# The instruction scheduler's simulator, exchanged under a two-layer diffusion block on one core

## Chip, cores and metric

The program runs on one core of a Trainium2 chip (trn2). The metric is the device time of one execution in microseconds (us). A run's time is that of the whole execution; a profiled execution has also a span, from its first to its last recorded instruction. The engines are PE (TensorE, matmuls; PEld is its weight load), DVE (VectorE), ACT (ScalarE), POOL (GpSimd) and SP (SyncE, which issues nearly all DMAs here). Each engine works through one list of instructions in the order in which the program holds them.

## The reference, cut to what matters

256 latent tokens `x` and 256 context tokens `ctx`, 1024 channels, go through two layers. In the last layer the context is only carried as far as its keys and values.

```python
for l in range(DEPTH):                                   # 2
    mod_x = silu(c) @ w_ada[l] + b_ada[l]                # 9 modulation vectors, also for ctx
    x = ffn_half(x, mod_x, 0, ...); cx = ffn_half(cx, ...)
    u_x, u_c = modulated_norm(x, ...), modulated_norm(cx, ...)
    q, k, v, f, cg, sc, g = split_in(u_x @ w_in[l])      # 18 tiles of branches, 32 of gates
    attn = latent_attention(...)                         # q/k RMS norm, rotary, softmax
    x = x + mod_x[5] * merge_branches(attn, f, cg, sc, g, lw)
    if not last: cx = cx + mod_c[5] * merge_branches(...)
    x = ffn_half(x, mod_x, 2, ...)                       # D_FF 2816
    if not last: cx = ffn_half(cx, ...)
return rmsnorm(x, final_norm_g)
```

`merge_branches` adds four gated branches: attention, a Fourier mixer, a convolution of 31 taps, a short gated convolution.

## The kernel before

Activations stand with channels on the 128 partitions and tokens along the free axis: 512 columns while both streams are carried (`NB = 2`: stream 0 latent, stream 1 context), 256 in the last layer's mixer and last FFN (`NB = 1`).

**Products.** Each f32 operand is split in a high and a low part. `mm3` (L192) issues three matmuls, at L193, L194 and L195, for high x high, high x low and low x high. `wblock` (L183) brings one weight block of 128 x 1024: a DMA by SP into a ring `raw` of 4 (L185), a cast by ACT into a ring `whi` of 6 (L187), a subtraction by DVE into a ring `wlo` of 6 (L189). `split` (L197) does the same for activations (L199 on ACT, L200 on DVE).

**Stages.** `ffn` (L559) runs first and second projection in three parts; `down` (L511) adds the result to the residual `xt`. In the last part its last two output tiles are computed stream by stream: stream 0's matmuls, then stream 1's, each followed by `residual` (L374 on DVE), `square_in` (L369 on ACT, L370 on DVE, into `acc`) and `nxt.stat(s)`. That statistic is `x_rstd`: narrow matmuls (L225) that sum squares over the channels, an inverse root of 11 small DVE instructions (`rsqrt`, L208 to L217), and a transpose that spreads it (L233). `Norm.part` (L415) then makes the next stage's input (L421 on DVE, L425 on ACT, L426 on DVE). The next stage's first products run by halves (`project(..., halves=True)`), so that stream 0 can begin while stream 1 is normalised. There are four such boundaries with two streams: FFN to mixer and mixer to FFN in layer 0, FFN to FFN between the layers, FFN to mixer in layer 1. Behind the layer 1 mixer stands a `LateNorm`, whose inverse root is multiplied in only behind the matmuls.

**Work between.** `ada_later` (L297) computes the later modulations on DVE (L331, L333, four instructions for each block of `w_ada`, ring of 2) and sums them with PE (L315). It is a generator that `filler` steps on inside FFN and merge. In the mixer, `attention` (L868) is another generator; the matmuls of scores are L888, the softmax is L892 (DVE), L895 (DVE), L900 (ACT), L903 and L904 (DVE), the transposes are L915 (PE) and L919 (ACT), the product with the values L932 (PE). `pump` and `tap` step attention and the convolution (L703, DVE) on between the gate products of `merge` (L991).

**What sets the order.** The Python program is traced in program order. Behind the trace, a list scheduler makes the order of every engine: it runs the program in a simulator, and whenever the simulated engine can take an instruction, it gives it the one that stands earliest in the program among those whose inputs are finished and whose ring slots are free in that simulation. The order found is written into the program and is the order on the chip; times of the simulation are not kept, only the order and the choice of ring slots, and semaphores are then assigned to it. Where the simulation and the chip differ, an engine on the chip can stand before an instruction that is not ready while a later one would be. Only the first piece of the program is fixed by hand, and only for two engines: `with tc.manual_schedule(engines={PE, SP})` at L1073, which takes in the loads of `x`, the first modulations and the first FFN products. Its ACT and DVE instructions are ordered by the scheduler as elsewhere.

The change touches the line that makes the context (L1264):

```python
    with tile.TileContext(nc) as tc:
        hybrid_block(tc, aps, out)
```

## Time and profile before

| what | value |
|---|---|
| median of 3 runs | 2047.06 us (2044.32 to 2049.98) |
| the profiled execution, its own time | 2047.93 us |
| its span | 2046.1 us |
| mean granted PE clock | 0.995 |
| instructions | 28,259 |
| DMA | 294.10 MB |

Busy time of an engine is the time in which at least one of its recorded instructions ran. A window row gives, for one stretch of the span, each engine's busy time with the number of instructions in brackets, then the granted clock of PE (1.00 is the full one), the share of time that the 16 DMA engines were busy, and their GB/s. In a timeline row the number in square brackets is the idle time of the engine ahead of the instruction and what ended it. In the chain of waits, each piece is the work that released the one behind it.

### The profile page before, as it was taken

Reading aid. Unit: us, or ns where it says so; the run is one execution under the profiler, and the core shown is the slowest. Engines: PE = TensorE matmul, PEld = TensorE weight load, DVE = VectorE, ACT = ScalarE, POOL = GpSimd, SP = SyncE. Lnnn points to the kernel's source line nnn. Section 1 sums busy time; section 2 is a strip of 40 time slices with the busy share of each in tenths; the row PEclk is TensorE's granted clock in tenths of the full one; section 3 lists DMA queues with packets and bytes.
Section 4 is the critical chain, followed back from the end, with each engine's and each line's share of the span. In section 5 each row is a group of like instructions: output and inputs, shape, how many; then the busy total and the mean of one; then the engine's idle time right before and its main releaser. Section 6 shows DMA issues by size and latency. Waiting matters only on the chain.

```text
span 2046.1 us, 28259 instructions
## 1 busy us (share of the span) xinstructions
PE 2006.9 (98%) x11074; PEld 1712.0 (84%) x11074; DVE 1376.6 (67%) x2470; ACT 737.0 (36%) x1142; POOL 5.1 (0%) x30
## 2 busy tenths in 40 slices
PE   6999999999999999999999999999999999999998
PEld 4878878888887778888887888888888999899997
DVE  5996697576766657768777657932424878767665
ACT  3322322333254442432222233222223545655443
POOL 0000000000000000000000000000000000000000
PEclk9999999999999999999999999999999999999999
DMA  8765566333222225246656533623323454446663
GB/s 295 232 204 168 159 212 193 111 96 98 83 86 84 78 70 167 75 153 192 198 160 192 165 101 109 220 83 95 111 87 101 140 165 140 139 125 205 181 182 92
DMA packets 83493, 294.10 MB, mean 144 GB/s; under 512 B 9504, under 2 KB 10144, under 8 KB 83360
## 3 DMA queue, kind: packets, MB, share of 16 engines
q1 hardware_dynamic: 83072, 292.07, 45.9%
q8 instruction: 87, 1.43, 0.3%
q14 instruction: 46, 0.38, 0.1%
q10 hardware_dynamic: 288, 0.23, 0.0%
HBM read 289.11 MB, written 1.05 MB: 142 GB/s over the span
## 4 chain that ended last, share of the span: by engine, by line
PE 95%; DVE 2%; ACT 1%; DMA 1%; issue 1%; DVEq 0%; ACTq 0%; SPq 0%
PE mm L193 30%; PE mm L194 30%; PE mm L195 29%; PE aux L932 1%; PE aux L888 1%; PE aux L915 1%; PE aux L315 1%; DVE wlo L189 1%; PE aux L775 1%; PE aux L225 0%; ACT whi L187 0%; PE aux L800 0%; DMA ada<-in_w_ada 0%; ACT s L900 0%; PE aux L260 0%
## 5 line engine op out<-in xcount | busy, mean ns | idle before, releaser
L193 PE MATMUL mm<-s,whi 128*128 128x512 f32 (+2 forms) x3354 | 1168.7, 349 | 4.8 <-ACT s L1003 1.4
L194 PE MATMUL mm<-s,whi 128*128 128x512 f32 (+2 forms) x3354 | 1165.3, 348 | 1.4 <-DVE s L200 1.2
L195 PE MATMUL mm<-s,wlo 128*128 128x512 f32 (+2 forms) x3354 | 1163.2, 347 | 0.0
L187 ACT CAST whi<-raw 128x1024 fp32r<-128x1024 f32 (+1 forms) x408 | 420.2, 1032 | 1051.4 <-PE mm L194 874.1
L189 DVE TENSOR_TENSOR wlo<-raw,whi 128x1024 fp32r<-128x1024 f32 (+1 forms) x408 | 487.1, 1199 | 347.1 <-ACT whi L187 331.3
L193 PEld LDWEIGHTS mm<-s,whi 128*128 128x128 f32 x3354 | 635.0, 190 | 101.1 <-ACT s L577 8.5
L194 PEld LDWEIGHTS mm<-s,whi 128*128 128x128 f32 x3354 | 636.6, 190 | 80.9 <-DVE s L200 2.1
L195 PEld LDWEIGHTS mm<-s,wlo 128*128 128x128 f32 x3354 | 636.2, 190 | 78.4 <-issue 0.8
L333 DVE SCALAR_TENSOR_TENSOR s<-ada,cw,s 128x512 f32<-128x512 f32 x448 | 307.4, 744 | 22.3 <-DMA ada<-in_w_ada 22.1
L374 DVE SCALAR_TENSOR_TENSOR xt<-mm,modG,xt 128x256 f32<-128x256 f32 x192 | 85.5, 478 | 132.9 <-PE mm L195 132.6
L199 ACT CAST s<-s 128x512 fp32r<-128x512 f32 (+1 forms) x104 | 59.4, 572 | 77.1 <-DVE s L587 48.9
L703 DVE SCALAR_TENSOR_TENSOR s<-pad,dw_h,s 128x512 f32<-128x512 f32 (+1 forms) x120 | 73.8, 615 | 2.1
L200 DVE TENSOR_TENSOR s<-s,s 128x512 fp32r<-128x512 f32 (+1 forms) x104 | 64.8, 623 | 2.0 <-ACT s L199 2.0
L425 ACT ACTIVATE s<-s,mod 128x256 fp32r<-128x256 f32 x80 | 39.4, 507 | 41.9 <-DVE s L421 41.8
L587 DVE TENSOR_TENSOR s<-s,mm 128x512 f32<-128x512 f32 x66 | 44.8, 680 | 1.2 <-ACT s L577 0.7
L892 DVE TENSOR_REDUCE sm<-aux 128x1 f32<-128x512 f32 (+1 forms) x48 | 28.6, 595 | 24.5 <-PE aux L888 24.4
L900 ACT ACTIVATE s<-aux,sm,sm 128x512 f32<-128x512 f32 (+1 forms) x48 | 34.0, 708 | 26.2 <-DVE sm L895 26.1
L467 DVE TENSOR_TENSOR s<-mm,s 128x256 f32<-128x256 f32 x44 | 18.1, 419 | 37.3 <-PE mm L195 37.3
L577 ACT ACTIVATE s<-mm 128x512 f32<-128x512 f32 x66 | 38.9, 590 | 1.2 <-PE mm L195 1.2
L426 DVE SCALAR_TENSOR_TENSOR s<-s,mod,s 128x256 fp32r<-128x256 f32 x80 | 37.2, 476 | 1.7 <-ACT s L425 1.7
L1024 DVE SCALAR_TENSOR_TENSOR s<-s,mm 128x512 f32<-128x512 f32 x48 | 32.7, 682 | 6.8 <-PE mm L195 5.9
L369 ACT ACTIVATE s<-xt 128x256 f32<-128x256 f32 x70 | 26.8, 410 | 28.2 <-DVE xt L374 28.1
(128 smaller groups left out, 723.0 us busy)
## 6 DMA issues: line engine op xcount, KB each, us to landing
raw<-in_w SPq DMA_DIRECT2D x208, 512.0 KB, 4.3
ada<-in_w_ada SPq DMA_DIRECT2D x144, 512.0 KB, 3.8
raw<-in_w_in SPq DMA_DIRECT2D x100, 512.0 KB, 3.7
raw<-in_w SPq DMA_DIRECT2D x64, 448.0 KB, 3.9
raw<-in_w_br SPq DMA_DIRECT2D x20, 512.0 KB, 3.6
raw<-in_w_o SPq DMA_DIRECT2D x16, 512.0 KB, 4.1
xt<-in_xt SPq DMA_DIRECT2D x4, 512.0 KB, 6.2
s<-s SPq DMA_DIRECT2D x16, 128.0 KB, 2.2
```

The lines of the kernel that those rows point to most:

```text
L187: nc.scalar.copy(hi[:, :n], raw[:, :n])
L189: nc.vector.tensor_tensor(out=lo[:, :n], in0=raw[:, :n], in1=hi[:, :n], op=ALU.subtract)
L193: nc.tensor.matmul(ps, lhsT=wh, rhs=xh, start=first, stop=False)
L194: nc.tensor.matmul(ps, lhsT=wh, rhs=xl, start=False, stop=False)
L195: nc.tensor.matmul(ps, lhsT=wl, rhs=xh, start=False, stop=last)
L199: nc.scalar.copy(hi[:, :n], src)
L200: nc.vector.tensor_tensor(out=lo[:, :n], in0=src, in1=hi[:, :n], op=ALU.subtract)
L333: nc.vector.scalar_tensor_tensor(out=t, in0=src, scalar=cs, in1=t, op0=ALU.mult, op1=ALU.add)
L374: nc.vector.scalar_tensor_tensor(out=xt[:, m, c], in0=ps[:, c], scalar=G[:, m, s : s + 1], in1=xt[:, m, c], op0=ALU.mult, op1=ALU.add,)
L425: nc.scalar.activation(hi[:, c], z, AF.Identity, bias=B[:, k, s : s + 1])
L587: nc.vector.tensor_tensor(out=h[:, :T], in0=s[:, :T], in1=ps[:, :T], op=ALU.mult)
L703: nc.vector.scalar_tensor_tensor(out=ov, in0=h[:, :NB, j : j + S], scalar=dw_h[:, l, i, j : j + 1], in1=ov, op0=ALU.mult, op1=ALU.add,)
```

## The change

One argument is given to the context; the body of the kernel is the same. With it, the scheduler drives another simulator: the library's timeline model of the devices in place of its default core simulator, each with its own durations and its own account of when an engine can take an instruction. The tracing, the priorities (the places in the program), the ring sizes and the region at L1073 are as they were.

```diff
@@ -1261,7 +1261,7 @@
     out = nc.dram_tensor("out", (P, KD, S), F32, kind="ExternalOutput").ap()
-    with tile.TileContext(nc) as tc:
+    with tile.TileContext(nc, schedule_with_timeline_sim=True) as tc:
         hybrid_block(tc, aps, out)
```

## Rows read from the trace of the kernel before

**Rows 1.** The page: busy time of the engines, with shares of the span.
```profile
PE 2006.9 (98%) x11074; PEld 1712.0 (84%) x11074; DVE 1376.6 (67%) x2470; ACT 737.0 (36%) x1142; POOL 5.1 (0%) x30
```

**Rows 2.** The page: the chain that ended last, shares of the span by engine.
```profile
PE 95%; DVE 2%; ACT 1%; DMA 1%; issue 1%; DVEq 0%; ACTq 0%; SPq 0%
```

**Rows 3.** Windows of the whole span, cut at the stage boundaries (columns in the first line).
```profile
core 0: us, PE busy (x) PEld busy (x) DVE busy (x) ACT busy (x) POOL busy (x), PEclk, DMA share, GB/s
0.00:45.00 45.00, 29.39 (x197) 19.11 (x198) 23.84 (x65) 17.60 (x33) 2.32 (x16) 1.00 0.80 291
45.00:404.00 359.00, 357.78 (x1633) 290.04 (x1634) 273.10 (x416) 99.50 (x134) 1.04 (x2) 1.00 0.60 188
404.00:604.00 200.00, 198.91 (x1019) 166.73 (x1018) 137.99 (x263) 74.51 (x116) 0.58 (x8) 1.00 0.29 89
604.00:850.00 246.00, 242.20 (x1187) 195.22 (x1185) 158.88 (x335) 103.89 (x193) 0.00 (x0) 0.99 0.33 99
850.00:862.00 12.00, 10.15 (x81) 9.66 (x81) 10.52 (x35) 6.20 (x13) 0.00 (x0) 1.00 0.13 44
862.00:1219.00 357.00, 356.15 (x1672) 292.95 (x1671) 252.31 (x387) 99.26 (x132) 0.00 (x0) 1.00 0.54 165
1219.00:1235.00 16.00, 14.58 (x106) 13.90 (x105) 12.45 (x47) 7.18 (x13) 0.00 (x0) 0.89 0.21 67
1235.00:1590.00 355.00, 355.00 (x1669) 295.34 (x1669) 174.91 (x256) 98.55 (x133) 0.00 (x0) 1.00 0.37 116
1590.00:1605.00 15.00, 13.57 (x96) 12.73 (x94) 11.67 (x44) 6.87 (x13) 0.00 (x0) 0.89 0.24 69
1605.00:1800.00 195.00, 192.68 (x1476) 180.76 (x1476) 157.91 (x319) 108.81 (x193) 1.17 (x4) 1.00 0.49 151
1800.00:2034.00 234.00, 234.00 (x1943) 233.73 (x1942) 157.66 (x293) 113.72 (x172) 0.00 (x0) 1.00 0.54 163
2034.00:2046.10 12.10, 2.51 (x17) 1.82 (x15) 5.30 (x18) 0.89 (x3) 0.00 (x0) 0.69 0.23 87
```

**Rows 4.** Windows of 10 us in the layer 0 mixer, around PE's longest stop there.
```profile
650.00:660.00 10.00, 6.34 (x28) 4.99 (x27) 6.47 (x12) 6.10 (x12) 0.00 (x0) 0.80 0.40 118
660.00:670.00 10.00, 10.00 (x50) 7.01 (x49) 5.50 (x18) 4.55 (x12) 0.00 (x0) 0.85 0.01 2
```

**Rows 5.** Timeline, 648 to 664 us, all engines: start, length, what, idle before.
```profile
651.29 1.05 ACT L187 CAST whi<-raw 128x1024 fp32r<-128x1024 f32 x1 [5.75 <-PE mm L194]
...
653.01 0.78 ACT L900 ACTIVATE s<-aux,sm,sm 128x512 f32<-128x512 f32 x1
...
655.55 0.66 PE L915 MATMUL aux<-ident,s 128*128 128x128 f32 x4 [2.72 <-DVE s L904]
```

**Rows 6.** Timeline of PE at the first two-stream boundary, 396 to 413 us.
```profile
404.64 0.61 PE L225 MATMUL aux<-ones_d,acc 128*128 128x1 f32 x4
...
408.55 0.28 PE L195 MATMUL mm<-s,wlo 128*128 128x256 f32 x1
408.75 1.05 PE L315 MATMUL aux<-s,ones_w 128*32 128x512 f32 x2
...
412.37 0.73 PE L193 MATMUL mm<-s,whi 128*128 128x256 f32 x4 [0.33 <-ACT s L425]
```

**Rows 7.** The chain of waits at that boundary, in order of time.
```profile
408.75 1.05 ACT whi L187
...
409.82 1.23 DVE wlo L189
411.05 0.35 DVE acc L370
```

**Rows 8.** Who waited for whom, ACT: total, times, longest.
```profile
ACT whi L187 <- PE mm L194: 874.1, 224, 17.3
```

**Rows 9.** The page's groups by line: the modulations' multiply-adds.
```profile
L333 DVE SCALAR_TENSOR_TENSOR s<-ada,cw,s 128x512 f32<-128x512 f32 x448 | 307.4, 744 | 22.3 <-DMA ada<-in_w_ada 22.1
```

**Rows 10.** Window in the first FFN of layer 1, nothing but wide products.
```profile
1350.00:1400.00 50.00, 50.00 (x222) 41.40 (x221) 15.48 (x20) 10.86 (x13) 0.00 (x0) 1.00 0.29 92
```

## The prediction

> **What bounds the kernel now.** I read the busy times first: PE is busy for 2006.9 us of the span of 2046.1, so it stands for only 39.2 us, while DVE has 67% and ACT 36% [rows 1]. The chain that ended last says the same, PE 95% [rows 2]. So the order of instructions can bring back no more than what PE stands, and what it loses in clock. The windows cut at the stage boundaries show where that is [rows 3]. The first stretch holds 45.00 - 29.39 = 15.6 us of it and the last one 12.10 - 2.51 = 9.6. The ten between hold 1.22 + 1.09 + 3.80 + 1.85 + 0.85 + 1.42 + 0 + 1.43 + 2.32 + 0 = 14.0 us. In the four long FFN stretches (45 to 404, 862 to 1219, 1235 to 1590, 1800 to 2034) PE stands 2.1 us out of 1305: there the reader is to see an engine that nothing holds up.
>
> **What the stops look like.** The longest is in the layer 0 mixer, and it is one of order. ACT reached a weight cast (L187) at 651.29 after 5.75 us of standing, since the cast needed a ring slot that PE's own matmuls had to free; the softmax of the attention (L900) stood behind it in ACT's list, and PE had already come to the transposes (L915) that need that softmax: 2.72 us [rows 5]. All in all PE lost 10.00 - 6.34 = 3.66 us in those 10 us, and the granted clock was 0.80 and then 0.85 over two windows of 10 us, another (0.20 + 0.15) x 10 = 3.5 us: 7.2 us for one misplaced hand-over [rows 4]. The casts stand 874.1 us behind PE, 224 times, up to 17.3 us [rows 8]; that costs something only where work that PE soon needs is queued behind one. The granted clock fell to 0.89 at two of the boundaries as well, 16 x 0.11 + 15 x 0.11 = 3.4 us [rows 3]. So the middle holds at most 14.0 + 3.5 + 3.4 = 20.9 us that a better order could give back.
>
> **The change, part by part.** It removes and adds no computation and no transfer: the same matmuls, casts and DMAs. What it can move is the place of each in the lists of ACT, DVE, PE, SP and POOL. POOL's 30 instructions (5.1 us) carry no weight [rows 1]. Five places count.
>
> - *The start.* PE's and SP's order is written by hand up to L1073's end; the stop of PE there stands ahead of the first products. Only ACT and DVE can be re-ordered, and they stand half empty (17.6 and 23.8 of 45.0 us) [rows 3]. I cost it at nothing, hidden by the wait for the loads of `x`; the cover lacks only if DVE put other work ahead of the square sums, one instruction of 744 ns [rows 9].
> - *The end.* One serial chain from the last matmul to the output, with nothing to choose between: nothing.
> - *The long FFN stretches.* Weight blocks run ahead through rings of 4 and 6, so a cast or a split that moves by a microsecond is covered by the blocks already there. Cost: nothing; gain at most 2.1 us. SP's list can swap a load of `w_ada` with one of a weight block; what covers that is the same rings, DMA being busy 0.37 to 0.60 of the time here [rows 3].
> - *The four boundaries with two streams.* This is the term. Before, the statistic of stream 0 (L225) was put into the middle of stream 1's matmuls, at 404.64, as soon as its sum was ready; stream 1 went on until 408.55, summing of modulations (L315) filled in from 408.75, and the next stage began at 412.37 [rows 6]. The slack is thus all used. If the new simulation lets PE's list take in the rest of stream 1's matmuls, which are ready, ahead of the statistic, it comes 408.55 - 404.64 = 3.9 us later, and everything of the next stage with it. The trace of before shows no boundary in that order, so I bound it: at least nothing or a small gain (an order better than before's could win back the 1.09 to 1.85 us that a boundary's stretch now stands), at most 3.9 us of standing and 3.5 us of clock behind it, as after the stop of 3.66 us [rows 4]. I take 3.9, near the middle, since the shorter stops at the boundaries took 1.7 us of clock or none [rows 3]. Four boundaries: **15.6 us**. Waiting on the statistic behind it are DVE's L421 and, through ACT's L425, PE's first products.
> - *The attention's hand-overs.* PE passes scores to DVE and ACT and takes the probabilities back. In the mixers PE stands 3.80 and 2.32 us in all [rows 3]. A new order moves these stops rather than ends them: I take nothing, between minus 7.2 us (the one large stop gone) and twice plus 7.2 (one more in each mixer) [rows 4].
>
> The sum is 15.6 us on the profiled execution: 2047.93 + 15.6 = 2063.5. That execution lies 0.87 us above the median shown, so the median becomes 2047.06 + 15.6 = **2062.7 us**.
>
> **Where the skill speaks for more.** In a stretch of nothing but wide products PE is busy 50.00 us of 50.00 and its weight load 41.40; 222 matmuls make 225 ns for each, against 213 ns for 512 columns at 2.4 GHz [rows 10]. PE waits for nothing in that stretch, so no order can shorten it. The Trainium skill (Trainium Kernel Development and Optimization, Performance Expectations) calls matmul busy time a bad measure of the distance to the roofline and the weight load's share a good one. By that reading 84% would leave 16% to win and the 20.9 us above would be no ceiling; the rows here do not bear that out for an exchange of order, and no term hangs on it.
>
> **The rivals.**
>
> *Faster.* The new simulation stands nearer to the chip and its order has fewer misplaced hand-overs. For it: at the boundary a cast of 1.05 us and a split of 1.23 stand ahead of the sum that the statistic waits for [rows 7], and at 651 the cast stood ahead of the softmax [rows 5]; an order that knew better would put both behind. Against it: the ceiling of 20.9 us, of which part is the latency of a serial chain that no order removes. I price it at half: 10.4 us, 2036.6. It decides if PE's stops at 650 and at 850, 1220 and 1590 are gone.
>
> *No change.* The two simulators order the same wherever it matters, or the change does nothing at all: 2047.1, within 0.3% (6 us, about what a measurement of this kernel can tell from no change). For it: 98% busy, and an order that follows the program wherever everything is ready.
>
> *Slower by more.* Work that is ready early but needed late is put ahead of a chain that PE waits for. The modulations' multiply-adds are that work: four of 744 ns make 3.0 us of DVE for each block [rows 9], and DVE is busy 10.52 of 12 and 12.45 of 16 us at boundaries [rows 3]. One block ahead of one hop at each boundary, with the 3.9 us, makes 4 x (3.9 + 3.0) = 27.6; two further stops in the mixers at 7.2 make 14.4: 42 us, 2089. It decides if DVE's L333 stands in the timeline between L374 and L208 at the boundaries.
>
> **How the numbers follow.** The forecast (the statistics late, 2062.7) has a chance of 0.32, the heavier rival 0.18, no change 0.25, faster 0.25. Why half the chance to lose: the gain has a ceiling of 1% and needs most of the stops mended, while the loss has none and needs one new stop at a place where the slack is used up. Faster by over 0.3% is then 0.25, within 0.3% 0.25, slower 0.50. The range goes from the middle of the faster case, 2036, to a little above the heavier one, 2092: half of the faster case and a part of the heavier lie outside, about 0.2. The slower cases alone run from 2053 to 2092.
>
> **What would show it.** Right: busy PE time about as now, and its idle time up by some 16 us, nearly all in the windows around the four boundaries; L225 of stream 0 behind the last of stream 1's matmuls in PE's timeline; the FFN stretches still full. Wrong: PE idle below 30 us and the mixer's stop at 650 gone (faster); the timeline of PE at the boundaries as now (no change); new stops of over 3 us with a granted clock below 0.9 in the mixers, or DVE's multiply-adds between residual and statistic (the heavier rival). Wrong altogether would be a stop in the FFN stretches: a weight ring run dry, casts or splits ordered too late, DMA waits in the chain.

## The result, and the profile after

| what | before | after |
|---|---|---|
| median of 4 runs each | 2048.52 us (2044.32 to 2050.73) | 2122.91 us (2121.66 to 2128.43) |
| ratio, 95% interval | | 1.0371 (1.0356 to 1.0386) |
| the profiled execution, its own time | 2047.93 us | 2121.66 us |
| its span | 2046.1 us | 2119.9 us |
| mean granted PE clock | 0.995 | 0.981 |

The change makes the kernel 3.7% slower, some 75 us. The forecast was slower by 15.6 us, with a range that ended at 2092: the direction was right and the size far too small.

The page of the kernel after, busy time of the engines (it answers to [rows 1]):

```profile
PE 2033.5 (96%) x11074; PEld 1731.4 (82%) x11074; DVE 1383.4 (65%) x2470; ACT 733.0 (35%) x1142; POOL 5.1 (0%) x30
```

Each engine's count of instructions is that of before. PE stood for 2119.9 - 2033.5 = 86.4 us against 39.2 before: 47.2 us more. The rest of the span's 73.8 us is PE's own busy time, 26.6 us more for the same 11074 matmuls, at a mean granted clock of 0.981 instead of 0.995.

Windows of 10 us of the kernel after, at the four boundaries, in the two mixers' worst places, with 50 us of an FFN among them (from 1300) and, as the last row, 20 us around the late norm behind the second mixer (columns as in [rows 3]: PE, PEld, DVE, ACT, POOL, then granted clock, DMA share, GB/s):

```profile
410.00:420.00 10.00, 5.25 (x32) 4.67 (x31) 9.16 (x29) 4.20 (x9) 0.00 (x0) 0.82 0.36 105
420.00:430.00 10.00, 10.00 (x74) 10.00 (x74) 6.95 (x25) 3.12 (x8) 0.00 (x0) 0.84 0.00 0
...
640.00:650.00 10.00, 5.61 (x31) 4.58 (x30) 5.34 (x14) 4.62 (x10) 0.00 (x0) 0.93 0.18 55
650.00:660.00 10.00, 6.42 (x18) 5.13 (x19) 5.73 (x12) 5.25 (x8) 0.00 (x0) 0.56 0.00 0
...
870.00:880.00 10.00, 8.72 (x74) 8.52 (x72) 5.11 (x15) 3.56 (x6) 0.00 (x0) 1.00 0.26 88
880.00:890.00 10.00, 6.81 (x30) 6.43 (x31) 9.01 (x31) 3.52 (x9) 0.00 (x0) 0.53 0.23 69
1250.00:1260.00 10.00, 9.45 (x80) 9.25 (x78) 6.26 (x14) 3.26 (x7) 0.00 (x0) 1.00 0.23 59
1260.00:1270.00 10.00, 5.89 (x26) 5.51 (x27) 9.04 (x32) 4.26 (x10) 0.00 (x0) 0.66 0.26 100
1300.00:1350.00 50.00, 50.00 (x209) 37.76 (x209) 46.10 (x68) 11.50 (x15) 0.00 (x0) 1.00 0.67 212
1630.00:1640.00 10.00, 7.49 (x63) 7.29 (x62) 6.22 (x17) 3.56 (x6) 0.00 (x0) 1.00 0.36 107
1640.00:1650.00 10.00, 7.54 (x41) 7.17 (x42) 8.54 (x33) 3.52 (x8) 0.00 (x0) 0.66 0.16 52
1790.00:1800.00 10.00, 4.74 (x24) 3.24 (x22) 6.50 (x20) 3.49 (x6) 0.00 (x0) 0.77 0.38 129
1800.00:1810.00 10.00, 9.44 (x59) 9.26 (x60) 7.77 (x19) 6.88 (x16) 0.00 (x0) 0.72 0.01 2
1920.00:1940.00 20.00, 15.20 (x107) 14.78 (x106) 13.38 (x34) 10.18 (x14) 0.00 (x0) 0.83 0.40 129
```

The reader is to see three things. The FFN is as full as before. At the four boundaries (the eight rows from 410, 420, 870, 880, 1250, 1260, 1630 and 1640) PE stands 4.75 + 0 + 1.28 + 3.19 + 0.55 + 4.11 + 2.51 + 2.46 = 18.9 us and the clock takes 10 x (0.18 + 0.16 + 0 + 0.47 + 0 + 0.34 + 0 + 0.34) = 14.9 us. Before, the same places held 1.85 + 1.42 + 1.43 us [rows 3] and 0.7 at the first one (PE was busy 19.34 of the 20 us from 404), 5.4 in all, and 3.4 us of clock [rows 3]. So the boundaries cost 13.5 us more in stops and 11.5 more in clock, 25 us of the span's 73.8. The other 49 us are what is left, nearly all of it in the mixers. The late norm behind the second one has 8 of them: 4.8 us of stops and 20 x 0.17 = 3.4 of clock in the last row.

Who waited for whom, PE of the kernel after (total us, times, longest):

```profile
PE aux L233 <- DVE sm L217: 22.8, 8, 3.5
...
PE mm L193 <- ACT s L1003: 13.1, 4, 8.0
PE aux L915 <- DVE s L904: 8.0, 8, 4.5
PE aux L915 <- ACT s L900: 4.5, 2, 2.3
...
PE mm L193 <- DVE sm L469: 2.3, 1, 2.3
PE aux L225 <- DVE acc L370: 1.5, 1, 1.5
```

The transposes behind an inverse root (L233) wait most, then, apart from the start (13.4 us, as before), gate products for a PSUM buffer (L1003) and the attention's transposes (L915).

PE and DVE at the first boundary, from the timeline of the kernel after (it answers to [rows 6]; for DVE, the last sum of stream 0 and its inverse root with what stands in it), and then that sum in the kernel before:

```profile
408.86 0.50 PE L225 MATMUL aux<-ones_d,acc 128*128 128x1 f32 x4
...
411.22 0.28 PE L195 MATMUL mm<-s,wlo 128*128 128x256 f32 x1
414.64 0.43 PE L233 MATMUL aux<-ident,sm 128*128 128x128 f32 x2 [3.15 <-DVE sm L217]
414.91 0.51 PE L225 MATMUL aux<-ones_d,acc 128*128 128x1 f32 x4
416.19 1.05 PE L193 MATMUL mm<-s,whi 128*128 128x256 f32 x4 [0.77 <-ACT s L425]
```

```profile
405.90 0.43 DVE L370 TENSOR_TENSOR acc<-acc,s 128x256 f32<-128x256 f32 x1 [0.54 <-ACT s L369]
...
409.40 0.16 DVE L208 TENSOR_SCALAR sm<-aux 128x2 f32<-128x2 f32 x1 [0.34 <-PE aux L225]
409.59 0.17 DVE L210 TENSOR_SCALAR sm<-sm 128x2 int32<-128x2 int32 x1
409.67 1.23 DVE L189 TENSOR_TENSOR wlo<-raw,whi 128x1024 fp32r<-128x1024 f32 x1
...
412.49 1.23 DVE L189 TENSOR_TENSOR wlo<-raw,whi 128x1024 fp32r<-128x1024 f32 x1
...
414.43 0.16 DVE L217 SCALAR_TENSOR_TENSOR sm<-sm,sm 128x2 f32<-128x2 f32 x1
```

```profile
404.16 0.42 DVE L370 TENSOR_TENSOR acc<-acc,s 128x256 f32<-128x256 f32 x1 [0.54 <-ACT s L369]
```

L225 of stream 0 comes at 408.86, before it came at 404.64: 4.2 us later. Only 2.5 us of that are its place in PE's list: its sum was ready at 406.33 (405.90 + 0.43), where before it was ready at 404.58 and L225 followed after 0.06 us; the other 1.7 us are a stage that came later as a whole. At the other three boundaries L225 runs 2.4 us behind its sum, where it was 0.05 to 0.06. Two weight splits of 1.23 us stand between the steps of the inverse root, where before there was one, and the root takes 5.2 us instead of 3.7. PE starts the last of stream 1's matmuls at 411.22 and the next stage's first product comes at 416.19 instead of 412.37. The summing of modulations (L315), which before filled the gap from 408.75, is used up here: in this trace it stands at 404.76.

The same hand-over in the layer 0 mixer: the convolution's layer norm, first as it was before, then after (PE's timeline):

```profile
615.55 0.95 PE L225 MATMUL aux<-ones_c,s 128*128 128x1 f32 x8
...
620.58 0.60 PE L233 MATMUL aux<-ident,sm 128*128 128x128 f32 x4
```

```profile
635.48 0.95 PE L225 MATMUL aux<-ones_c,s 128*128 128x1 f32 x8
...
644.14 0.60 PE L233 MATMUL aux<-ident,sm 128*128 128x128 f32 x4
...
653.58 0.80 PE L193 MATMUL mm<-s,whi 128*128 128x512 f32 x1 [7.97 <-ACT s L1003]
```

From the statistic to its transposes it was 5.0 us, now 8.7; in the kernel after, DVE's last step of the inverse root ran at 641.44, so the result lay ready for 2.5 us while PE went through products that stood ahead. Behind the transposes come three steps on DVE and three on ACT for each half, from 644.97 until ACT's last one ends at 652.95, and ACT's evacuation of a gate product (L1003, at 652.86) stands behind them in ACT's list, as it did before. Before, PE still had products to do meanwhile: it was busy 24.94 of the 25 us from 612 to 637. After, it had done them already: counted in PE's instructions as they ran, 2494 product matmuls (those into `mm`) stand ahead of this statistic before and 2544 after, and 50 of them at 225 ns [rows 10] are about 11 us, as an estimate. The way from the statistic to the end of the last ACT step is no longer than before (17.5 us; before 17.8, from 615.55 to 633.33). What is gone is the work that covered it, and PE stood 7.97 us for the PSUM buffer: the longest stop behind the start, with a granted clock of 0.56 in the window that holds its end.

### The profile page after: what moved, and what is told of

The parts are those of the page before. It is cut to its first block, busy times and chain, and to the rows that moved or that the text cites. A ratio compares the mean times of both kernels' runs of the same rounds, so it can differ in the third digit from the quotient of the medians.

```text
span 2119.9 us, 28318 instructions
## 1 busy us (share of the span) xinstructions
PE 2033.5 (96%) x11074; PEld 1731.4 (82%) x11074; DVE 1383.4 (65%) x2470; ACT 733.0 (35%) x1142; POOL 5.1 (0%) x30
## 3 DMA queue, kind: packets, MB, share of 16 engines
q8 instruction: 87, 1.43, 0.3%
## 5 line engine op out<-in xcount | busy, mean ns | idle before, releaser
L193 PE MATMUL mm<-s,whi 128*128 128x512 f32 (+2 forms) x3354 | 1170.0, 352 | 26.3 <-ACT s L1003 13.1
L194 PE MATMUL mm<-s,whi 128*128 128x512 f32 (+2 forms) x3354 | 1171.8, 350 | 2.8 <-DVE s L426 2.8
L193 PEld LDWEIGHTS mm<-s,whi 128*128 128x128 f32 x3354 | 639.5, 192 | 128.7 <-ACT s L1003 15.0
L195 PEld LDWEIGHTS mm<-s,wlo 128*128 128x128 f32 x3354 | 642.8, 192 | 82.7 <-issue 4.5
L194 PEld LDWEIGHTS mm<-s,whi 128*128 128x128 f32 x3354 | 643.1, 192 | 82.2 <-DVE s L426 4.2
L189 DVE TENSOR_TENSOR wlo<-raw,whi 128x1024 fp32r<-128x1024 f32 (+1 forms) x408 | 486.9, 1202 | 330.2 <-ACT whi L187 292.0
L333 DVE SCALAR_TENSOR_TENSOR s<-ada,cw,s 128x512 f32<-128x512 f32 x448 | 308.6, 750 | 37.3 <-DMA ada<-in_w_ada 37.1
L199 ACT CAST s<-s 128x512 fp32r<-128x512 f32 (+1 forms) x104 | 59.4, 571 | 138.0 <-DVE s L587 96.8
L200 DVE TENSOR_TENSOR s<-s,s 128x512 fp32r<-128x512 f32 (+1 forms) x104 | 65.2, 627 | 17.7 <-ACT s L199 17.7
L900 ACT ACTIVATE s<-aux,sm,sm 128x512 f32<-128x512 f32 (+1 forms) x48 | 34.0, 708 | 34.9 <-DVE sm L895 31.0
L587 DVE TENSOR_TENSOR s<-s,mm 128x512 f32<-128x512 f32 x66 | 45.0, 682 | 0.7 <-ACT s L577 0.7
L919 ACT COPY s<-aux 128x256 f32<-128x256 f32 x80 | 26.3, 378 | 43.8 <-PE aux L915 43.7
L915 PE MATMUL aux<-ident,s 128*128 128x128 f32 x160 | 26.9, 294 | 12.4 <-DVE s L904 8.0
```

The lines of the kernel that those rows point to most:

```text
L189: nc.vector.tensor_tensor(out=lo[:, :n], in0=raw[:, :n], in1=hi[:, :n], op=ALU.subtract)
L193: nc.tensor.matmul(ps, lhsT=wh, rhs=xh, start=first, stop=False)
L194: nc.tensor.matmul(ps, lhsT=wh, rhs=xl, start=False, stop=False)
L195: nc.tensor.matmul(ps, lhsT=wl, rhs=xh, start=False, stop=last)
L199: nc.scalar.copy(hi[:, :n], src)
L200: nc.vector.tensor_tensor(out=lo[:, :n], in0=src, in1=hi[:, :n], op=ALU.subtract)
```

## The experiments

Two theories were set against each other at the start. **W**: PE's list holds ready products ahead of statistics and transposes that were not yet ready, since the new simulator hands an engine instructions far ahead (a parameter of the library's model, its issue window, which is 35 instructions for PE and 12 for each other engine). The rival, **D**: the new model's durations change the choices of ACT and DVE, or of all engines, and PE's place is only a result of that. Where an order is held, the program is traced twice: the first trace gives each engine's list, and in the second each instruction is tied to the one that is to stand ahead of it, without a semaphore. The edits are shortened where they hold an order.

**Is it order at all?** The changed kernel with the lists of PE, ACT, DVE and SP held to the order of before; POOL's few instructions are left to the new simulator.

```diff
-    with tile.TileContext(nc, schedule_with_timeline_sim=True) as tc:
-        hybrid_block(tc, aps, out)
+    _, order = _build(arrays, timeline=False)
+    nc, _ = _build(arrays, timeline=True, engines=(PE, Activation, DVE, SP), order=order)
...
+        for engine in engines:
+            for a, b in zip(order[engine], order[engine][1:]):
+                tc.add_manual_dep(named[b], a, NoSync)
```

> The timeline model runs, but PE, ACT, DVE and SP are all held to the order of the kernel before; only POOL's 27 instructions and whatever else the model decides (ring slots, semaphores) are its own. Theory O (the loss is the order and nothing else): 2040 to 2052 us. Theory S (part of the loss is in the ring slots or semaphores that come with the model): over 2060 us.

Measured: 2047.05 us, 1.0002 (0.9992 to 1.0012). The whole loss is the order; what else the new simulator could have changed (ring slots, semaphores) costs nothing that shows.

**PE's list alone, both ways.** The timeline model with PE's list of before, and the default simulator with PE's list of after.

```diff
-    with tile.TileContext(nc, schedule_with_timeline_sim=True) as tc:
+    _, order = _build(arrays, timeline=False)
+    nc, _ = _build(arrays, timeline=True, engines=(PE,), order=order)
```

> The scheduler simulates with the timeline model, but PE's instructions are held to the order that they have in the kernel before; ACT, DVE, SP and POOL are ordered by the timeline model. Theory W (the loss is PE's order: the model's issue window lets ready matmuls in ahead of the narrow hand-over matmuls): back to 2040 to 2060 us, idle of PE 35 to 50 us against 86.4 in the changed kernel. Theory D (the loss is in the order of DVE and ACT, of whose 2462 and 1091 instructions 1590 and 386 stand at another place): 2100 us or more.

```diff
-    with tile.TileContext(nc) as tc:
+    _, order = _build(arrays, timeline=True)
+    nc, _ = _build(arrays, timeline=False, engines=(PE,), order=order)
```

> The mirror image: the default simulator orders ACT, DVE, SP and POOL, while PE's instructions are held to the order that they have in the changed kernel. Theory W: 2105 to 2130 us, the whole loss. Theory D: under 2070 us.

Measured: 2106.76 us, 1.0298 (1.0277 to 1.0320), and 2112.93 us, 1.0327 (1.0311 to 1.0342). PE's list of after makes nearly the whole loss under the simulator of before, as W said; but PE's list of before doesn't mend the kernel after, which W had at 2040 to 2060; there D, with 2100 or more, was right, and in the mirror image, with under 2070, it was wrong. The waits on PE of the kernel with PE held to before:

```profile
...
PE aux L225 <- DVE acc L370: 10.1, 6, 4.0
PE aux L233 <- DVE sm L217: 7.9, 6, 2.2
PE mm L194 <- DVE s L200: 6.3, 2, 3.2
...
PE mm L193 <- ACT s L199: 5.6, 6, 2.2
```

These are other stops than those of the kernel after, two of them (L200, L199) within an FFN, where DVE went through eight multiply-adds of modulations (L333, 5.39 us at 251.59) ahead of the product (L587) whose split PE needed. So holding one engine's list doesn't isolate that engine: DVE's and ACT's lists are chosen under it, and lists from two schedules need not fit each other, as here. The two parts, 1.0298 and 1.0327, add up to far more than the whole.

**The issue window.** The changed kernel, with the parameter for PE set to 12 and to 4, then for PE, DVE and ACT to 4, 2 and 2.

```diff
+    from concourse.hw_specs import TRN2Spec
+    TRN2Spec.ENG_ISSUE_QUEUE_DEPTH[mybir.EngineType.PE] = 12
     with tile.TileContext(nc, schedule_with_timeline_sim=True) as tc:
```

> The changed kernel with one parameter of the timeline model set: the issue window of PE is 12 instructions in place of 35; all else is as in the changed kernel. Theory W: the narrow matmuls come some 4 to 11 places late in place of 11 to 35, so a third of the loss, 2060 to 2085 us. Theory D: 2110 us or more, since the DVE order still differs in 1435 places.

```diff
+    TRN2Spec.ENG_ISSUE_QUEUE_DEPTH[mybir.EngineType.PE] = 4
```

> The same with an issue window of PE of 4 instructions. Theory W: the loss is gone, 2040 to 2058 us. Theory D: 2110 us or more, since the DVE order still differs in 1340 places.

```diff
+    TRN2Spec.ENG_ISSUE_QUEUE_DEPTH[mybir.EngineType.PE] = 4
+    TRN2Spec.ENG_ISSUE_QUEUE_DEPTH[mybir.EngineType.DVE] = 2
+    TRN2Spec.ENG_ISSUE_QUEUE_DEPTH[mybir.EngineType.Activation] = 2
```

> The timeline model with issue windows of 4 for PE and of 2 for ACT and DVE (35, 12 and 12 as shipped). With 4 for PE alone it was 2089 us. Theory W2 (the rest of the loss is the same effect in DVE's and ACT's lists, weight splits let in ahead of the small instructions of a chain): 2050 to 2070 us. Theory D (the rest is the model's durations): 2080 to 2095 us, as with PE's window alone.

Measured: 2101.14 us, 1.0268 (1.0253 to 1.0284); 2089.12 us, 1.0210 (1.0195 to 1.0225); 2078.36 us, 1.0153 (1.0135 to 1.0171). A shorter window wins at each step, 1.0371 to 1.0153, and PE's window alone gives back (1.0371 - 1.0210) x 2048.5 = 33 us. The traces show what it does to PE's list. Take each narrow matmul of a statistic (L225), a spreading transpose (L233), the scores (L888) and the attention's transposes (L915) by its rank among those of its line, and count the product matmuls (into `mm`) ahead of it: in the kernel after there are on average 24 to 29 more than before, by line, with a window of 12 it is 9 to 14, with 4 it is 4 to 5, with 4, 2 and 2 it is 5 to 9. But W had more for each of the first two times, and 2078.4 lies between what W2 and D had: the window is a large part of the cause, 45 of the 76 us, not all of it. The waits on PE with windows of 4, 2 and 2:

```profile
...
PE aux L233 <- DVE sm L217: 12.8, 7, 3.0
PE mm L193 <- ACT s L1003: 5.2, 2, 3.4
PE aux L225 <- DVE acc L370: 3.3, 2, 1.7
```

The longest stop behind the start went from 8.0 to 3.4 us, the wait at L233 from 22.8 to 12.8. About 31 us are left against before. Cut at the same matmuls of PE's list, the traces (28.5 us apart) have 11 of them at the four boundaries, 7 in the layer 1 mixer and none in the layer 0 mixer.

**Where.** The changed kernel with only the two mixers' instructions held to the order of before, and with all but those.

```diff
+    nc, _ = _build(arrays, timeline=True, engines=(PE, Activation, DVE, SP), order=order, stages="mixers")
...
+            kept = [n for n in order[engine] if stages is None or (n in mixers) == (stages == "mixers")]
+            for a, b in zip(kept, kept[1:]):
```

> The same pins, but only for the instructions traced between the first group of products of a mixer and its last projection, in both mixers; FFNs and the four stage boundaries are ordered by the timeline model. From the windows of the changed kernel, about 52 us of its loss (idle and clock) are in the mixers and 25 at the boundaries: 2122 less about 50, 2060 to 2085 us. If the boundaries carry the most, 2100 us or more.

```diff
+    nc, _ = _build(arrays, timeline=True, engines=(PE, Activation, DVE, SP), order=order, stages="rest")
```

> The complement: FFNs and boundaries held to the order of the kernel before, the middle of the two mixers ordered by the timeline model. 2122 less about 25, 2085 to 2105 us; if the boundaries carry the most, under 2075 us.

Measured: 2080.35 us, 1.0160 (1.0144 to 1.0176), and 2095.35 us, 1.0230 (1.0210 to 1.0250). Holding the mixers wins 0.0211 of the ratio, 43 us, holding the rest 0.0141, 29 us; together 72 of 76, so here the parts do add up; that a stage's lists come from one schedule is the likely reason. It agrees with the windows to some 4 us: the late norm stands behind the second mixer's last projection and was held with the rest, so they have 49 - 8 = 41 us in the mixers and 25 + 8 = 33 outside. The wait of L193 for L1003, 13.1 us with only the rest held, is 1.0 with the mixers held, where L233 still waits 19.7.

**The filled chain.** The next theory, C, took the picture at 409 to 414 us at its word: work put between the steps of an inverse root delays what PE waits for. All lists are held, and in DVE's the 11 steps of every inverse root are put together, what stood between coming behind them: in the order of after, of the small windows, and of before.

```diff
+        links.update({n: chain for n in chain})
+    kept, done = [], set()
+    for n in order:
+        for m in links.get(n, [n]):
+            if m not in done:
+                done.add(m)
+                kept.append(m)
+    return kept
...
+    order[dve] = _closed(order[dve])
```

> All four engines are held to the changed kernel's order, except that in DVE's list the 11 instructions of each inverse root stand together, and what stood between them (24 weight splits of 1.23 us, softmax pieces, normalisation) comes right behind. Theory C (the holes of a dependent chain, which the new simulator fills with ready work, are what PE waits for): at each of the four boundaries about two splits leave the chain, 4 x 2.5, and in the mixers the layer norm's chains lose up to 10 softmax instructions of 0.8 us, so 2085 to 2105 us, with PE's waits at L233 for L217 down from 22.8 us to under 12. Theory R (the order is late elsewhere, in PE's list itself, and the wait only changes its name): 2113 to 2124.

> The order found with the issue windows 4, 2 and 2 (2078.4 us), all four engines held to it, with the inverse roots' instructions together in DVE's list. Theory C: what the small windows left is in good part the filled holes (21 splits stand in the chains, two each at three boundaries, and 10 to 18 other instructions in four chains), so 2058 to 2070 us and the 12.8 us at L233 for L217 about halved. Theory R: 2074 to 2080.

> The order of before, all four engines held to it, with the inverse roots together. Nine splits stand in its chains, none of them two at a time but at one place, and stream 1's chains have the ten normalisations of stream 0 between their steps, which now come up to 2 us later. Theory C: little is to be had here, and the ten moved normalisations are what PE begins the next stage with: 2042 to 2056 us. If every hop of a chain that is shortened paid: 2035 to 2041.

Measured: 2132.55 us, 1.0403 (1.0385 to 1.0420); 2086.08 us, 1.0187 (1.0171 to 1.0202); 2063.27 us, 1.0074 (1.0059 to 1.0089). All three are slower than the orders they were made from, and slower than any of the expectations had it. These orders were held under the default simulator; the order of after held so without a change was not run, so the comparison with 2122.9 takes it that holding costs nothing, which is shown for the order of before alone, under the new simulator. The waits on PE of the first:

```profile
...
PE mm L194 <- DVE s L426: 11.0, 4, 3.1
PE aux L233 <- DVE sm L217: 9.3, 7, 2.2
PE aux L225 <- DVE acc L370: 9.1, 5, 2.9
```

The wait at L233 did fall as C said, from 22.8 to 9.3. But the wait of the next stage's products for their normalised input (L194 for L426) rose from 2.8 to 11.0: the ten normalisations of stream 0 that stood between stream 1's steps now came behind them (with these left in their place, in the next runs, it is 2.6). And the wait of L225 for the sum rose from 1.5 to 9.1. To take the first of these out, the same again with L421 and L426 left where they stood:

```diff
+        others = [n for n in inside if n not in chain and not at(n, 421) and not at(n, 426)]
+        order = order[:first] + [n for n in inside if n not in others] + others + order[last + 1 :]
```

> All four engines held to the changed kernel's order; in DVE's list everything that stood between the steps of an inverse root comes behind it, but for the normalisations L421 and L426, which stay where they were (closing the chains over these as well cost 11 us of waiting at L194 for L426 in the run before). Theory C' (weight splits and softmax pieces between the steps delay what PE waits for, the normalisations between them do not): about 2.5 us at each of four boundaries, 2105 to 2116 us. Theory R (the time of a chain's steps is not what PE lacks, the holes are filled for free): 2119 to 2127.

> The same mend on the order found with the issue windows 4, 2 and 2 (2078.4 us as found, 2086.1 with the chains closed altogether). Theory C': 2062 to 2072 us, PE's waits at L233 for L217 down from 12.8 us to under 5 with nothing new at L194. Theory R: 2076 to 2088.

Measured: 2125.50 us, 1.0380 (1.0364 to 1.0396), and 2082.57 us, 1.0169 (1.0153 to 1.0184): no better than 1.0371 and 1.0153, and both where theory R had them. In the first of the two the waits at L233 and at L225 are 9.3 and 9.1 us as in the run before. In the second L233 waits 3.3 us instead of 12.8 and L194 for L426 only 0.4, just what C' asked for, but L225 waits 11.8 for L370 instead of 3.3.

Theory C falls as an account of the time. The splits in the chain are there and the wait at L233 ends last behind them; but with them gone, 13.5 us at L233 become 7.6 us at L225 for L370 and stops elsewhere. Over the same matmuls of PE's list, the first of the two stands 15.0 us at the four boundaries instead of 18.8, and their stretches are 2 us shorter, where C' had about 10; the two mixers are 3 us longer. The splits and sums between the steps have to be done in any case, and what is moved behind one chain can stand ahead of the next.

**One hand-over of before.** In the order of before, the softmax (L900) and the cast L860 ahead of it are moved ahead of the two weight casts that stood before them at 651 us [rows 5].

```diff
+    queue = order[act]
+    for i in range(len(queue) - 4):
+        if [at(n, l) for n, l in zip(queue[i:], (187, 187, 860, 900))] == [True] * 4:
+            queue[i : i + 4] = [queue[i + 2], queue[i + 3], queue[i], queue[i + 1]]
```

> The order of before, all four engines held to it, with one hand-over in ACT's list exchanged: at 651 us the softmax (L900) and the cast L860 ahead of it now stand before the two weight casts that waited for PE. Theory F (that stop and the clock behind it were the 7.2 us that the rows around 650 show): 2038 to 2044 us. Theory G (the weight blocks then come late, or the second half of the softmax is the next wait): 2045 to 2051.

Measured: 2051.01 us, 1.0019 (1.0010 to 1.0028): where theory G had it. ACT, DVE and PE there, from the timeline:

```profile
649.91 0.62 ACT L860 CAST s<-s 64x512 fp32r<-64x512 f32 x1 [10.32 <-PE mm L194]
650.56 0.78 ACT L900 ACTIVATE s<-aux,sm,sm 128x512 f32<-128x512 f32 x1
...
651.33 2.92 ACT L187 CAST whi<-raw 128x1024 fp32r<-128x1024 f32 x3
```

```profile
652.39 2.36 DVE L189 TENSOR_TENSOR wlo<-raw,whi 128x1024 fp32r<-128x1024 f32 x2 [11.58 <-ACT whi L187]
...
656.17 0.48 DVE L904 TENSOR_SCALAR s<-s,sm 128x512 f32<-128x512 f32 x1
```

```profile
656.70 0.69 PE L915 MATMUL aux<-ident,s 128*128 128x128 f32 x2 [5.92 <-DVE s L904]
```

L860 itself waits 10.32 us for PE's L194 here, so the softmax behind it gained little: it came 11.6 us behind the L860 before (638.97), where it was 12.0 in the order of before (653.01 behind 640.98). What cost the time is DVE's list, which was held as it was: the splits of two of the moved casts stand in it ahead of the last steps of the softmax. DVE stood 11.58 us for those casts and split until 654.75, L904 came at 656.17, and PE's stop at L915 is 5.92 us instead of 2.72. The row of DVE in the kernel before shows the same hold there: its split of the cast of 651.29 stands from 652.37 ahead of L903 and L904. So the exchange doesn't show what the softmax alone, ahead of casts and splits in both lists, would have given; that was not tried.

**No window.** To see whether the 31 us that are left are still the window, it was set to 1 for all five engines.

```diff
+    TRN2Spec.ENG_ISSUE_QUEUE_DEPTH[mybir.EngineType.PE] = 1
...
+    TRN2Spec.ENG_ISSUE_QUEUE_DEPTH[mybir.EngineType.Pool] = 1
     with tile.TileContext(nc, schedule_with_timeline_sim=True) as tc:
```

> The changed kernel with the simulator's issue window at 1 for all five engines, so that the simulated engine is never given an instruction before it can begin it. Windows of 35 and 12, as they are, gave 2122.9 us, of 4, 2 and 2 for PE, DVE and ACT 2078.4. Theory W (what is left is still the window): 2050 to 2066 us. Theory D (what is left comes from the simulator's durations, which make another work ready at each choice): 2070 to 2082.

Measured: 2233.59 us, 1.0909 (1.0886 to 1.0931), which neither theory had. The waits on PE:

```profile
PE aux L233 <- DVE sm L217: 25.2, 12, 4.9
PE aux L915 <- DVE s L904: 20.8, 21, 4.2
PE mm L193 <- ACT s L199: 20.1, 5, 8.2
...
PE aux L888 <- DMA s<-s: 13.1, 1, 13.1
PE mm L193 <- DVE s L587: 9.9, 3, 6.4
```

There are stops everywhere, the FFNs included (L199, L587). So a shorter window isn't better without end. By the same count as above, the narrow matmuls now stand too early: L225, L233, L888 and L915 have on average 6, 12, 13 and 26 product matmuls fewer ahead of them than before, and L233 and L915 head the list of PE's waits. That their early place is what makes these waits is likely, but was not tested by itself. SP's and POOL's windows were changed here as well, and which of the five does it was not tried. What the 31 us are that remain at 4, 2 and 2 stays open: hardly the filled chains, and whether the model's durations, what is left of the window, or the windows of SP and POOL was not told apart.

## Why the prediction was wrong

- *The order is the whole effect, and the FFNs stay full.* Right: 1.0002 with the lists held, and 50.00 of 50 us in the FFN after. The start and the end were rightly taken at nothing: PE's wait for the first sum of squares (L225 for L1082) is 13.4 us after and 13.9 before, and from the last statistic to the end it is 9.9 us after and 9.3 before.
- *The four boundaries, 15.6 us.* The mechanism was there, but smaller than it was priced: L225 of stream 0 stands 12 product matmuls later in PE's list at the first boundary and 21 at the other three, still within stream 1's matmuls and not behind the last, and runs 2.4 to 2.5 us behind its sum, where 3.9 was taken. That the stops of this term came to 13.5 us all the same, near the 15.6, is in part luck: at the first boundary the inverse root was 1.5 us longer and the summing (L315) that had covered the wait was used up, and neither was in the sum. What failed is the choice of no clock behind them: the bound named 3.5 us for each, the text took 0 "since the shorter stops at the boundaries took 1.7 us of clock or none", and the runs show 11.5 us over the four, 2.9 for each. Each boundary's stops of 4.5 to 5.0 us went with 3.4 to 4.7 us of clock here, as 3.66 us went with 3.5 in [rows 4]. With that the term is 25.0 where it was 15.6.
- *The attention's hand-overs, 0 us.* This is the step that made the miss: 43 us by the held mixers, 41 by the windows without the late norm, against a bound of 14.4. The late norm's 8 us were in no term at all. The sentence that failed is "A new order moves these stops rather than ends them". It counted the stops that were there, 6.1 us, and not the hand-overs that had been covered. What I said of the boundary's statistic (ready products taken in ahead of it) held for nearly all hand-overs of the mixers too: 152 of the 160 matmuls of L915 and 92 of the 96 of L888 have more product matmuls ahead of them than before. The layer norm's two statistics in layer 0 have 32 and 50 more, and 7.97 us of standing came from that one place. The boundary's mechanism had to be counted at all hand-overs, not at the four that I had looked at.
- *The rivals.* The heavier one, at 2089 and 0.18, was nearest, and for part of its reasons: stops of over 3 us with a clock below 0.9 in the mixers are what the windows at 640 to 660 and 1790 to 1810 show. Its other half, multiply-adds (L333) ahead of the chain at the boundaries, is not there; splits (L189) are, and taking them out won nothing in the time.
- *The faster rival.* It was to be decided by the stops at 650 and at the boundaries, and they are not gone but longer. Its reading of the hand-over at 651 was right as ACT's list goes and left out DVE's, where the split of the same cast stands ahead of the softmax's last steps. The exchange in ACT's list alone cost 3.7 us instead of giving 7.2; it doesn't show that a better order at that place would win nothing.
- *Busy time as a measure.* The Trainium skill (Trainium Kernel Development and Optimization, Performance Expectations) prefers the weight load's share to matmul busy time. Nothing here tells the two apart: for the same 11074 matmuls both grew, PE by 26.6 us and the weight load by 19.4, while both shares of the span fell, 98% to 96% and 84% to 82%. It wasn't what the prediction failed on.

## What to carry to other kernels

In a kernel whose slowest engine is 98% busy, count the hand-overs that are covered, not the stops that are left: each is a place where a new order can lose, and the stops of the present trace bound only the gain. Price a new stop with the clock behind it. When an order is to be tested by holding it, hold all engines over a stage; here the list of one engine from one schedule under the lists of another measured their misfit as well, and an exchange in one engine's list has to be followed through the lists that wait for it.

## What was not expected of the hardware

- At each of the four boundaries PE stood 4.5 to 5.0 us in all, and a window of 10 us there or right behind has a granted clock between 0.53 and 0.84; 0.53 is nearly the whole window at 1.2 GHz instead of 2.4. Before, stops of 1.4 us went with 0.89 at two of the boundaries, and one of 1.85 us with 1.00 at the third [rows 3]. PE's mean clock went from 0.995 to 0.981, and PE's busy time for the same matmuls rose by 26.6 of the 73.8 us.
- A wait that was removed came back under another name more than once: 22.8 us of L233 for L217 became 9.3 with the chains closed, while L225 for L370 rose by 7.6, and the time didn't fall.
